# A decoder block in three-pass float32 matmuls: high and low halves share a tile, and gap tiles set their addresses

## The chip, the core and the metric

The kernel runs on one core of a Trainium2 chip. The metric is the device time of one execution in microseconds. A core has a matrix engine (TensorE, PE in the profile), a vector engine (VectorE, DVE), an activation engine (ScalarE, ACT), a general engine (GpSimd, POOL) and a queue that issues transfers (SyncE, SP). TensorE multiplies a stationary operand, the weights, which a separate step loads (PEld in the profile), with a moving operand that streams past it. Both are read from SBUF, the on-chip memory of 128 partitions; the result goes to PSUM, from which the other engines read it.

## The reference, cut to what matters

One layer of a decoder for 256 prompt tokens and 8 x 4 sample tokens, 288 in all, with a width of 2048. Everything is float32.

```python
mod = silu(c) @ w_ada + b_ada                      # shifts, scales, gates
h = rmsnorm(x, norm1) * (1 + sc1) + sh1
proj = h @ w_in                                    # 2048 -> 4632
u_pool, z, xbc, dt_raw = split(proj)
mix = concat(pool_mixer(u_pool), ssd_mixer(z, xbc, dt_raw)) @ w_out
x = x + g1 * mix
h2 = rmsnorm(x, norm2) * (1 + sc2) + sh2
up = h2 @ w_up                                     # 2048 -> 2 x 5504
act = silu(causal_dwconv(up[:, :5504])) * up[:, 5504:]
x = x + g2 * (act @ w_down)
y = rmsnorm(x, norm_f)                             # and the new states
```

## The kernel before, in words

The data lie transposed: features on the partitions, the 288 tokens along the row. A width of 2048 is 16 tiles of 128 x 288. [...] Each factor is split into a high half, rounded to float32r, and a low half, the rest. Then `mm3` (lines 222 to 226) adds three products into one PSUM bank: high weights by high operand (L224), high weights by low operand (L225), low weights by high operand (L226). Every pass has its own weight load of 128 x 128 and streams 288 columns.

The operands that move are h1 (for the input projection), mix (for the output projection) and h2 (for up); `new_operand` (lines 179 to 181) makes 16 high tiles under one tag and 16 low tiles under another, in the pool `kp`. The 43 activation tiles for down are made one by one in `up_pair` (lines 1024 to 1027), with 17 buffers for the high and 17 for the low halves.

Weights come from DRAM in pieces of 128 x 1024 on SP's queue (`load`, line 208). `split` (lines 214 to 220) makes two tiles of each piece: ACT casts it into `whi` (L218), DVE subtracts that from the piece into `wlo` (L219). The class `_W` (line 363) hands out the buffers in turn. The first pool has two of each, and a second pool adds two more of each in the output projection, when the mixer's memory has come free. A piece holds 8 blocks of 128 x 128, so it serves 24 matmuls.

Order of the stages: c and x in, the first norm; the modulation weights and the input projection (`xbc`, then `dt` with blocks of 24 columns, then `uz`), with the mixers' work woven in; the output projection (`out`); the second norm; the first three pairs of columns of up, k by k (`up`, 18 matmuls for each k); then 40 pairs `gate` and `val`, of 48 matmuls each, and in three groups `down`. A tile framework sets the semaphores: it knows which part of a tile an instruction reads or writes, and a new tile in an old buffer waits until the old one is released. A scheduler orders each engine's instructions from the dependencies and its own estimates; work marked with high priority, such as the casts and subtractions of `split`, goes ahead.

Addresses are dealt out by the pools, one tile after the other. An operand tile takes 1152 bytes of each partition, a piece of split weights 4096, a block of it 512.

Of the kernel before, what the change touches and what calls it, by code (L numbers as in the profile page):

```python
# [11 lines left out]
F32 = mybir.dt.float32  # L12
F32R = mybir.dt.float32r
# [4 lines left out]
P = 128  # L18
D = 2048
KT = D // P  # L20
# [3 lines left out]
N = NP + NS  # L24
# [13 lines left out]
WU = (14, 2, 2, 2, 6)  # L38
RAW1, RAW2 = 8, 1
SPLIT1, SPLIT2 = 2, 2  # L40
YK = 2
NX = (10, 1, 1, 1, 1)
AY = 2
# [14 lines left out]
RAWC = 1024  # L58
# [73 lines left out]
def kernel(ctx: ExitStack, tc, ins, outs):  # L132
# [4 lines left out]
    kp = ctx.enter_context(tc.tile_pool(name="kp", bufs=1))  # L137
# [38 lines left out]
    xhi = [None]  # L176
    xlo = [None]

    def new_operand(name):
        xhi[0] = [kp.tile([P, N], F32R, tag="xhi", name=f"{name}h{k}", bufs=KT) for k in range(KT)]  # L180
        xlo[0] = [kp.tile([P, N], F32R, tag="xlo", name=f"{name}l{k}", bufs=KT) for k in range(KT)]

    def col_sums(ps, src, rhs, first, last):

# [21 lines left out]
    wp = [None]  # L206

    def load(key):
        off, cols = S.items[key]
        t = wp[0].tile([P, RAWC], F32, tag="raw", name="raw_" + "_".join(map(str, key)))  # L210
        nc.sync.dma_start(t[:, :cols], wflat[off:off + P * cols].rearrange("(p n) -> p n", p=P))
        return t

    def split(raw, a, n, name):
        hi = wp[0].tile([P, RAWC], F32R, tag="whi", name="whi_" + name)
        lo = wp[0].tile([P, RAWC], F32R, tag="wlo", name="wlo_" + name)
        with tc.high_priority():
            nc.scalar.copy(hi[:, :n], raw[:, a:a + n])  # L218
            nc.vector.tensor_tensor(lo[:, :n], raw[:, a:a + n], hi[:, :n].bitcast(F32), ALU.subtract)  # L219
        return hi, lo  # L220

    def mm3(ps, whi, wlo, c, bh, bl, first, last, n=P):
        w = slice(c * n, c * n + n)
        nc.tensor.matmul(ps, whi[:, w], bh, start=first, stop=False)  # L224
        nc.tensor.matmul(ps, whi[:, w], bl, start=False, stop=False)  # L225
        nc.tensor.matmul(ps, wlo[:, w], bh, start=False, stop=last)  # L226
# [3 lines left out]
    def project_units(key, nk, opnd=None, order=None):  # L230

        name = "_".join(map(str, key))
        ps = pm.tile([P, 512], F32, tag="mm", name="mm_" + name)
        for h, (k0, n) in enumerate(_halves(nk)):
            hi, lo = ready.pop(key + (h,), None) or split(load(key + (h,)), 0, n * P, f"{name}_{h}")
            for i in range(n):
                k = k0 + i
                ko = order[k] if order else k
                bh, bl = (xhi[0][ko], xlo[0][ko]) if opnd is None else opnd(k)
                mm3(ps[:, :N], hi, lo, i, bh, bl, k == 0, k == nk - 1)  # L240
                if k % YK == YK - 1 or k == nk - 1:
                    yield ps

    def project(key, nk, opnd=None, order=None):
        for ps in project_units(key, nk, opnd, order):
            pass
        return ps
# [93 lines left out]
    def samp(ap):  # L341
        return ap.rearrange("p (b l) -> p b l", b=NB)
# [20 lines left out]
    class _W:  # L363


        def __init__(self):
            self.slots = {"raw": [], "whi": [], "wlo": []}
            self.i = {"raw": 0, "whi": 0, "wlo": 0}

        def add(self, pool, nraw, nsp):  # L370
            for tag, n in (("raw", nraw), ("whi", nsp), ("wlo", nsp)):
                m = len(self.slots[tag])
                if m:
                    r = self.i[tag] % m
                    self.slots[tag] = self.slots[tag][r:] + self.slots[tag][:r]
                    self.i[tag] = 0
                self.slots[tag] += [(pool, n)] * n
# [11 lines left out]
    for q in range(4):  # L389
        t = mx.tile([P, 4, N], F32, tag="blk", name=f"xa{q}", bufs=4)  # L390
# [36 lines left out]
    nc.vector.memset(upp[:, :, 0:15], 0.0)  # L427

    new_operand("h1")

    selr = mx.tile([P, 32], F32R, name="selr")
# [415 lines left out]
    for gi in range(len(KGROUPS)):  # L847
        last = gi + 1 == len(KGROUPS)
        if last:
            hi, lo = split(load(("dt",)), 0, KT * NH, "dt")  # L850
# [23 lines left out]
    n = 0  # L874
    zlast = 3 * (4 - ZEARLY) * KT // YK
    for m in list(range(4 + 3 * ZEARLY, 16)) + ULATE:
# [22 lines left out]


    new_operand("mix")
    def mix_pool(g):
        nc.scalar.copy(xhi[0][g], pout[0][:, g, :])
        nc.vector.tensor_tensor(xlo[0][g], pout[0][:, g, :], xhi[0][g].bitcast(F32), ALU.subtract)

    for g in range(4):
        for t in range(3):
            k = 4 + 3 * g + t
# [7 lines left out]
    ff = ctx.enter_context(tc.tile_pool(name="ff", bufs=1, reuse_waits="tile"))  # L916
    w2 = ctx.enter_context(tc.tile_pool(name="w2", bufs=1, reuse_waits="tile"))
    x = ff.tile([P, KT, N], F32, name="x")


    rt = [kp.tile([P, N], F32, tag="ssx", name="rt2")]
# [60 lines left out]
    for _ in range(GA[1]):  # L982
        next(adag2)
    new_operand("h2")
    up0 = [(pm.tile([P, 512], F32, tag="mm", name=f"mm_up{i}") if i < 3 else aux(f"mm_up{i}"))
           for i in range(2 * FK)]
    for k0, n in [(0, 1), (1, 1)] + [(k, 2) for k in range(2, KT, 2)]:
        modulate(x[:, k0:k0 + n, :], rstd2 if k0 > 1 else rstd2p, 1, 3, k0, n, f"n{k0}")
        for k in range(k0, k0 + n):
            hi, lo = ready.pop(("upk", k), None) or split(load(("upk", k)), 0, 2 * FK * P, f"upk{k}")  # L990
# [9 lines left out]
    def up_pair(j):  # L1000
        pg = up0[2 * j] if j < FK else project(("gate", j), KT)
        gb = ff.tile([P, NG], F32, tag="gb", name=f"gb{j}", bufs=2)
        gs = gb[:, 2 + NP:].rearrange("p (b l) -> p b l", b=NB)
        nc.gpsimd.memset(gb[:, 0:2], 0.0)
        nc.gpsimd.tensor_copy(gs[:, :, 0:2], stf[:, j])
        nc.scalar.copy(gb[:, 2:2 + NP], pg[:, 0:NP])
        nc.scalar.copy(gs[:, :, 2:6], samp(pg[:, NP:N]))
        nc.gpsimd.tensor_copy(nff[:, j, 0:2], gb[:, NP:NP + 2])
        nc.gpsimd.tensor_copy(nff[:, j, 2:18].rearrange("p (b l) -> p b l", b=NB), gs[:, :, 4:6])
        fw = V_FW + 3 * j  # L1010
        gc = ff.tile([P, NG], F32, tag="gc", name=f"gc{j}", bufs=2)
        nv = NG - 2
        nc.vector.tensor_scalar(gc[:, :nv], gb[:, 0:nv], vec[:, fw:fw + 1], vec[:, V_FB + j:V_FB + j + 1],
                                ALU.mult, ALU.add)
        for i in (1, 2):
            nc.vector.scalar_tensor_tensor(out=gc[:, :nv], in0=gb[:, i:i + nv], scalar=vec[:, fw + i:fw + i + 1],
                                           in1=gc[:, :nv], op0=ALU.mult, op1=ALU.add)
        nc.scalar.activation(gc[:, :nv], gc[:, :nv], AF.Silu)
        pv = up0[2 * j + 1] if j < FK else project(("val", j), KT)
        act = ff.tile([P, N], F32, tag="act", name=f"act{j}", bufs=2)  # L1020
        nc.vector.tensor_tensor(act[:, 0:NP], gc[:, 0:NP], pv[:, 0:NP], ALU.mult)
        gcs = gc[:, 2 + NP:].rearrange("p (b l) -> p b l", b=NB)[:, :, 0:NL]
        nc.vector.tensor_tensor(samp(act[:, NP:N]), gcs, samp(pv[:, NP:N]), ALU.mult)
        ah = ff.tile([P, N], F32R, tag="ah", name=f"ah{j}", bufs=17)
        al = ff.tile([P, N], F32R, tag="al", name=f"al{j}", bufs=17)
        nc.scalar.copy(ah, act)  # L1026
        nc.vector.tensor_tensor(al, act, ah.bitcast(F32), ALU.subtract)
        acts[j] = (ah, al)
# [39 lines left out]
    xf = [None]  # L1068

    def down(gi):  # L1070
        k0, nk = DGROUPS[gi]
        last = gi == len(DGROUPS) - 1
        for m in range(16):
            for i, ps in enumerate(project_units(("down", gi, m), nk, lambda k: acts[k0 + k])):
                if last and m == KT - 1 and i == 5:
                    all_but_last("ssumf")
            residual(ps, 5, m)
            if last:
                squares(m, "f")
                nc.scalar.activation(xf[0][m], x[:, m, :], AF.Identity, scale=vec[:, V_NF + m:V_NF + m + 1])  # L1080

    for gi, (k0, nk) in enumerate(DGROUPS):
        for j in range(k0, k0 + nk):
            up_pair(j)
            if gi == 0 and j >= 3:
                next(adag2, None)
                next(adag2, None)
            if j >= SM0:
                next(states, None)
            if gi and j == k0:  # L1090
                drain(adag2)
                down(gi - 1)
    drain(states)
    nc.gpsimd.dma_start(outs["o_ffn"], nff)
    rt[0] = kp.tile([P, N], F32, tag="ssx", name="rtf")
    xf[0] = [kp.tile([P, N], F32, tag="xhi", name=f"xf{m}", bufs=KT) for m in range(KT)]
    down(len(DGROUPS) - 1)


# [161 lines left out]
```

## Time and profile before

| | us |
|---|---|
| median of 3 runs | 1391.12 |
| the runs | 1389.8 to 1391.21 |
| span of the profiled execution | 1387.7 |
| median of the runs less that span | 3.4 |
| TensorE busy | 1363.0 (98%) |
| weight loads | 1252.7 (90%) |
| DVE, ACT, POOL busy | 823.0, 576.7, 228.6 |

The span runs from the first to the last instruction of the profiled execution; a run's time also holds what lies around that, so a sum against the span is carried over with the 3.4 us. A matmul's end is modelled, and matmuls overlap in the records (each is listed with some 295 ns, and the next starts some 133 ns later). So the rate of a stage is read from the distance between starts. The timeline prints starts to 10 ns; the trace holds whole nanoseconds, and means over many starts are given to a hundredth.

### The profile page before, as it was taken

The numbers are of one execution on the slowest core, as the hardware profiler recorded it, in microseconds if no ns is written. First come the engines' busy times: TensorE is split into PE (matmuls) and PEld (weight loads), VectorE is DVE, ScalarE is ACT, GpSimd is POOL, SyncE is SP. The second block draws the span as 40 slices with busy tenths as digits, with TensorE's granted clock in tenths as the row PEclk, the third lists the DMA queues.
The fourth block names the chain that finished last, engine by engine and source line by source line (L and its number), as shares of the span: only waits on it lengthen the run. The fifth ranks groups of instructions, "written<-read, shape, count | busy, mean of one in ns | idle before, by whom it ended". The sixth has DMA issues, their size and how long they took to land.

```text
span 1387.7 us, 26411 instructions
## 1 busy us (share of the span) xinstructions
PE 1363.0 (98%) x10565; PEld 1252.7 (90%) x10565; DVE 823.0 (59%) x1448; ACT 576.7 (42%) x925; POOL 228.6 (16%) x428
## 2 busy tenths in 40 slices
PE   8999999999989999999999999999999999999997
PEld 7678888777679998998999999999999999999997
DVE  3775657968774447745565445665664565565553
ACT  5222333479653334533443333434433334343452
POOL 0000000121122223111221001312120012122221
PEclk9999999999999999999999999999999999999999
DMA  8888887978788887788655555655555555556531
GB/s 340 306 296 306 307 283 253 340 278 326 296 310 316 332 286 245 219 290 280 217 180 175 170 173 180 199 190 188 180 179 167 181 191 190 188 187 197 188 118 68
DMA packets 97194, 323.20 MB, mean 233 GB/s; under 512 B 10736, under 2 KB 19888, under 8 KB 97072
## 3 DMA queue, kind: packets, MB, share of 16 engines
q1 hardware_dynamic: 93168, 310.63, 65.6%
q0 software_dynamic: 3184, 9.69, 1.9%
q8 instruction: 83, 1.36, 0.4%
q10 hardware_dynamic: 720, 1.19, 0.2%
q14 instruction: 39, 0.32, 0.1%
HBM read 309.78 MB, written 10.39 MB: 231 GB/s over the span
## 4 chain that ended last, share of the span: by engine, by line
PE 94%; DVE 3%; DMA 1%; ACT 1%; issue 0%; POOL 0%; SPq 0%; DVEq 0%; POOLq 0%; ACTq 0%
PE mm_down L224 7%; PE mm_down L226 7%; PE mm_down L225 7%; PE mm_gate L226 6%; PE mm_gate L224 6%; PE mm_val L225 6%; PE mm_gate L225 6%; PE mm_val L226 6%; PE mm_val L224 6%; PE xbc L224 5%; PE xbc L225 4%; PE xbc L226 4%; PE adap L322 3%; PE mm_out L224 3%; PE mm_out L225 3%; PE mm_out L226 2%
## 5 line engine op out<-in xcount | busy, mean ns | idle before, releaser
L224 PE MATMUL mm_down<-ah,whi_down 128*128 128x288 f32 x688 | 203.7, 296 | 0.0
L226 PE MATMUL mm_down<-ah,wlo_down 128*128 128x288 f32 x688 | 203.5, 296 | 0.0
L225 PE MATMUL mm_down<-al,whi_down 128*128 128x288 f32 x688 | 203.3, 295 | 0.0
L226 PE MATMUL mm_gate<-h2h,wlo_gate 128*128 128x288 f32 x640 | 190.2, 297 | 0.0
L224 PE MATMUL mm_gate<-h2h,whi_gate 128*128 128x288 f32 x640 | 189.8, 297 | 0.0
L225 PE MATMUL mm_gate<-h2l,whi_gate 128*128 128x288 f32 x640 | 189.3, 296 | 0.0
L225 PE MATMUL mm_val<-h2l,whi_val 128*128 128x288 f32 x640 | 188.8, 295 | 0.0
L226 PE MATMUL mm_val<-h2h,wlo_val 128*128 128x288 f32 x640 | 188.5, 295 | 0.0
L224 PE MATMUL mm_val<-h2h,whi_val 128*128 128x288 f32 x640 | 188.0, 294 | 0.0
L219 DVE TENSOR_TENSOR wlo_gate<-raw_gate,whi_gate 128x1024 fp32r<-128x1024 f32 x80 | 98.5, 1232 | 138.7 <-ACT whi_gate L218 138.6
L219 DVE TENSOR_TENSOR wlo_down<-raw_down,whi_down 128x1024 fp32r<-128x1024 f32 x96 | 107.9, 1123 | 116.8 <-ACT whi_down L218 116.0
L218 ACT CAST whi_down<-raw_down 128x1024 fp32r<-128x1024 f32 x96 | 92.2, 961 | 169.2 <-PE mm_down L225 119.2
L218 ACT CAST whi_gate<-raw_gate 128x1024 fp32r<-128x1024 f32 x80 | 83.9, 1050 | 163.4 <-PE mm_gate L225 68.8
L224 PE MATMUL xbc<-h1h,whi_xbc 128*128 128x288 f32 x448 | 139.9, 313 | 4.6 <-DVE cvp L553 2.9
L218 ACT CAST whi_val<-raw_val 128x1024 fp32r<-128x1024 f32 x80 | 84.1, 1051 | 125.6 <-issue 102.3
L225 PE MATMUL xbc<-h1l,whi_xbc 128*128 128x288 f32 x448 | 132.4, 296 | 0.3 <-DVE h1l L360 0.3
L226 PE MATMUL xbc<-h1h,wlo_xbc 128*128 128x288 f32 x448 | 131.8, 297 | 0.0
L225 PEld LDWEIGHTS mm_down<-al,whi_down 128*128 128x128 f32 x688 | 129.7, 189 | 0.0
L226 PEld LDWEIGHTS mm_down<-ah,wlo_down 128*128 128x128 f32 x688 | 129.6, 188 | 0.0
L224 PEld LDWEIGHTS mm_down<-ah,whi_down 128*128 128x128 f32 x688 | 129.6, 188 | 0.0
L224 PEld LDWEIGHTS mm_gate<-h2h,whi_gate 128*128 128x128 f32 x640 | 120.4, 188 | 5.0 <-ACT ah L1026 3.4
L225 PEld LDWEIGHTS mm_gate<-h2l,whi_gate 128*128 128x128 f32 x640 | 120.7, 189 | 0.0
(318 smaller groups left out, 3003.6 us busy)
## 6 DMA issues: line engine op xcount, KB each, us to landing
raw_adap<-wflat SPq DMA_DIRECT2D x128, 512.0 KB, 5.6
raw_gate<-wflat SPq DMA_DIRECT2D x80, 512.0 KB, 3.5
raw_val<-wflat SPq DMA_DIRECT2D x80, 512.0 KB, 3.6
raw_ada<-wflat SPq DMA_DIRECT2D x64, 512.0 KB, 5.6
raw_xbc<-wflat SPq DMA_DIRECT2D x55, 512.0 KB, 5.8
raw_down<-wflat SPq DMA_DIRECT2D x48, 512.0 KB, 3.6
raw_out<-wflat SPq DMA_DIRECT2D x32, 512.0 KB, 7.0
raw_down<-wflat SPq DMA_DIRECT2D x32, 384.0 KB, 3.1
```

What stands on the lines that cost most here:

```text
L218: nc.scalar.copy(hi[:, :n], raw[:, a:a + n])
L219: nc.vector.tensor_tensor(lo[:, :n], raw[:, a:a + n], hi[:, :n].bitcast(F32), ALU.subtract)
L224: nc.tensor.matmul(ps, whi[:, w], bh, start=first, stop=False)
L225: nc.tensor.matmul(ps, whi[:, w], bl, start=False, stop=False)
L226: nc.tensor.matmul(ps, wlo[:, w], bh, start=False, stop=last)
L322: i = nc.tensor.matmul(ps[32 * j:32 * j + 32, :512], sc_c[:, k, :], raw[:, (j % 2) * 512:(j % 2) * 512 + 512], start=(k == ay - 1), stop=( ...
```

## The change

Nothing is computed in another way. `new_operand` makes 16 tiles of 128 x 2 x 288, the high half first; `up_pair` does the same for the activations. `split` makes one tile of 2048 + 64 columns for a piece, with the high half at column 0 and the low half at column 1024 + 32. `_W` has one list of buffers for it in place of two. `shift` takes a small unused tile from a pool, so that what the pool deals out afterwards lies 192 bytes (pool `kp`, operands), 32 bytes (pool `ff`, activations) or 0 bytes (second weight pool) further on. The tiles of the final norm use the operands' buffers as before, under the new tag.

```diff
+PHASE = (192, 32, 0)
...
+    def shift(pool, n, name):
+        if n:
+            pool.tile([P, n // 4], F32, name="gap_" + name)
+
+    shift(kp, PHASE[0], "x")
+
     def new_operand(name):
-        xhi[0] = [kp.tile([P, N], F32R, tag="xhi", name=f"{name}h{k}", bufs=KT) for k in range(KT)]
-        xlo[0] = [kp.tile([P, N], F32R, tag="xlo", name=f"{name}l{k}", bufs=KT) for k in range(KT)]
+        pair = [kp.tile([P, 2, N], F32R, tag="xop", name=f"{name}k{k}", bufs=KT) for k in range(KT)]
+        xhi[0] = [t[:, 0, :] for t in pair]
+        xlo[0] = [t[:, 1, :] for t in pair]
...
     def split(raw, a, n, name):
-        hi = wp[0].tile([P, RAWC], F32R, tag="whi", name="whi_" + name)
-        lo = wp[0].tile([P, RAWC], F32R, tag="wlo", name="wlo_" + name)
+        pair = wp[0].tile([P, 2 * RAWC + 64], F32R, tag="wsp", name="wsp_" + name)
+        hi, lo = pair[:, 0:RAWC], pair[:, RAWC + 32:2 * RAWC + 32]
...
-        for tag, n in (("raw", nraw), ("whi", nsp), ("wlo", nsp)):
+        for tag, n in (("raw", nraw), ("wsp", nsp)):
...
+    shift(ff, PHASE[1], "a")
+    shift(w2, PHASE[2], "w")
...
-        ah = ff.tile([P, N], F32R, tag="ah", name=f"ah{j}", bufs=17)
-        al = ff.tile([P, N], F32R, tag="al", name=f"al{j}", bufs=17)
+        ahl = ff.tile([P, 2, N], F32R, tag="ahl", name=f"ahl{j}", bufs=17)
+        ah, al = ahl[:, 0, :], ahl[:, 1, :]
```

Two places show what this does to the instructions. The first is DVE, in the middle of gate and val, with the semaphores that each instruction waits for. Before (`wlo` is the low half of a piece of weights, `gc` the convolved gate, `act` its product with val):

```order
L219 TENSOR_TENSOR wlo_gate_0_9912<-raw_gate_0_9909,whi_gate_0_9911 128x1024 [waits DMAHW3_49,PE_49,Activation_49]
L219 TENSOR_TENSOR wlo_gate_1_9942<-raw_gate_1_9939,whi_gate_1_9941 128x1024 [waits DMAHW4_49,PE_49,Activation_49]
L1013 TENSOR_SCALAR gc_9831<-gb_9824,vec 128x304 [waits Activation_49]
L1016 SCALAR_TENSOR_TENSOR gc_9831<-gb_9824,vec,gc_9831 128x304 [waits DVE_49] x2
L219 TENSOR_TENSOR wlo_val_0_9985<-raw_val_0_9982,whi_val_0_9984 128x1024 [waits DMAHW5_49,PE_49,Activation_49]
L1021 TENSOR_TENSOR act_9897<-gc_9831,mm_val_9836 128x256 [waits PE_49,Activation_49]
```

The same place in the changed kernel, where high and low half are parts of one tile `wsp`:

```order
L228 TENSOR_TENSOR wsp_gate_0_9633<-raw_gate_0_9631,wsp_gate_0_9633 128x1024 [waits DMAHW3_49,Activation_49]
L228 TENSOR_TENSOR wsp_gate_1_9662<-raw_gate_1_9660,wsp_gate_1_9662 128x1024 [waits DMAHW4_49,Activation_49]
L1024 TENSOR_SCALAR gc_9556<-gb_9549,vec 128x304 [waits Activation_49]
L1027 SCALAR_TENSOR_TENSOR gc_9556<-gb_9549,vec,gc_9556 128x304 [waits DVE_49] x2
L228 TENSOR_TENSOR wsp_val_0_9704<-raw_val_0_9702,wsp_val_0_9704 128x1024 [waits DMAHW5_49,Activation_49]
L1032 TENSOR_TENSOR act_9620<-gc_9556,mm_val_9561 128x256 [waits PE_49,Activation_49]
```

The order is the same. The subtraction no longer waits for TensorE, since the cast ahead of it on ACT has waited for the release of the whole tile.

The second place is ACT, late in the input projection, around the step that makes dt (`csd`, `ex`, `etb`, `csr` belong to it, `cf` to the convolution). Before:

```order
L218 CAST whi_xbc_6_2849<-raw_xbc_6_2847 128x1024 [waits DMAHW3_49,Activation_49]
L506 ACTIVATE csd<-csd 128x72 [waits DVE_49]
L510 ACTIVATE ex<-csd 128x24
L511 ACTIVATE ex<-cumt 128x24 [waits PE_49]
L521 ACTIVATE etb<-totb 128x192 [waits PE_49]
L527 CAST csr<-cumr 24x288 [waits PE_49]
L218 CAST whi_xbc_7_2889<-raw_xbc_7_2887 128x1024 [waits DMAHW4_49,PE_49,Activation_49]
L570 ACTIVATE cf_3141<-cvp_161,vec 128x312 x4
L218 CAST whi_xbc_8_2945<-raw_xbc_8_2943 128x1024 [waits DMAHW1_49,DVE_49,PE_49]
```

And in the changed kernel:

```order
L227 CAST wsp_xbc_6_2784<-raw_xbc_6_2782 128x1024 [waits DMAHW3_49,DVE_49,PE_49]
L515 ACTIVATE csd<-csd 128x72 [waits DVE_49]
L519 ACTIVATE ex<-csd 128x24
L520 ACTIVATE ex<-cumt 128x24 [waits PE_49]
L227 CAST wsp_xbc_7_2823<-raw_xbc_7_2821 128x1024 [waits DMAHW4_49,PE_49,Activation_49]
L530 ACTIVATE etb<-totb 128x192
L536 CAST csr<-cumr 24x288
L579 ACTIVATE cf_3070<-cvp_162,vec 128x312 x5
L227 CAST wsp_xbc_8_2878<-raw_xbc_8_2876 128x1024 [waits DMAHW1_49,DVE_49,PE_49]
```

Here the cast of piece 7 has moved two places ahead, and the cast of piece 6 waits for PE and DVE, the readers of the whole tile whose buffer it takes. From the second column of the output projection to the end TensorE has the same order in both kernels; the moves lie in the input projection, and a few single ones on ACT and DVE behind it.

More of the change, by code (lines that the diff above doesn't have):

```diff
@@ L366, in __init__ @@
         def __init__(self):
-            self.slots = {"raw": [], "whi": [], "wlo": []}
-            self.i = {"raw": 0, "whi": 0, "wlo": 0}
+            self.slots = {"raw": [], "wsp": []}
+            self.i = {"raw": 0, "wsp": 0}
         def add(self, pool, nraw, nsp):
-            for tag, n in (("raw", nraw), ("whi", nsp), ("wlo", nsp)):
+            for tag, n in (("raw", nraw), ("wsp", nsp)):
                 m = len(self.slots[tag])
@@ L1095 @@
     rt[0] = kp.tile([P, N], F32, tag="ssx", name="rtf")
-    xf[0] = [kp.tile([P, N], F32, tag="xhi", name=f"xf{m}", bufs=KT) for m in range(KT)]
+    xf[0] = [kp.tile([P, N], F32, tag="xop", name=f"xf{m}", bufs=KT) for m in range(KT)]
     down(len(DGROUPS) - 1)
```

## The prediction

> **What bounds the kernel now.** The page comes first: the busy times, and the chain of work that ended last.
>
> ```profile
> span 1387.7 us, 26411 instructions
> PE 1363.0 (98%) x10565; PEld 1252.7 (90%) x10565; DVE 823.0 (59%) x1448; ACT 576.7 (42%) x925; POOL 228.6 (16%) x428
> PE 94%; DVE 3%; DMA 1%; ACT 1%; issue 0%; POOL 0%; SPq 0%; DVEq 0%; POOLq 0%; ACTq 0%
> ```
>
> TensorE sets the end: 98% busy and 94% of the chain. The table of stretches says where anything else could count.
>
> ```profile
> 50.00:330.00 280.00, 275.17 (x2197) 219.39 (x2197) 195.60 (x452) 111.97 (x181) 27.20 (x47) 1.00 0.83 299
> 640.00:1000.00 360.00, 360.00 (x2706) 357.40 (x2706) 206.33 (x297) 139.61 (x196) 60.14 (x130) 1.00 0.59 191
> 1000.00:1388.00 388.00, 378.19 (x2843) 377.73 (x2841) 215.11 (x327) 153.25 (x220) 69.36 (x131) 0.99 0.53 168
> ```
>
> From 640 to 1000 us TensorE is never idle (360.00 of 360.00) at a granted clock of 1.00; in the input projection, 50 to 330 us, it lacks 4.8 us. Since it is always busy, "busy" says nothing about how fast it goes. That is read from the start-to-start distance, the pitch, in the timeline. Here two neighbouring matmuls of a "val" tile, with the weight loads beside them:
>
> ```profile
> 1200.32 0.29 PE L224 MATMUL mm_val<-h2h,whi_val 128*128 128x288 f32 x1
> 1200.32 0.19 PEld L225 LDWEIGHTS mm_val<-h2l,whi_val 128*128 128x128 f32 x1
> 1200.45 0.30 PE L225 MATMUL mm_val<-h2l,whi_val 128*128 128x288 f32 x1
> 1200.45 0.19 PEld L226 LDWEIGHTS mm_val<-h2h,wlo_val 128*128 128x128 f32 x1
> ```
>
> The load of the next weights starts with the matmul before it: while TensorE streams a moving operand, it fetches the weights of the following one from the same memory. That is the pair whose distance the change sets. L224 to L226 run 2912 times each, 8736 matmuls. In 8569 cases one is followed by another; 8397 of these lie under 150 ns apart, and their mean pitch is 132.74 ns, 1114.6 us of the span.
>
> **Does the pitch depend on that distance?** Call the offset the byte address of the next weights minus that of the moving operand, modulo 256. An operand tile is 288 x 4 = 1152 bytes, 4.5 x 256, so neighbouring tiles flip the offset by 128; a block of weights is 512 bytes, so it does not move. From the allocator's addresses, the weight buffers of the first pool give 64 and 192 with h1, mix and h2, those of the second 96 and 224; in "down" the two pools give 224/96 and 0/128. The four offsets that stand still over 18 matmuls are in the first columns of up, one k after the other:
>
> ```profile
> 552.60 0.30 PE L224 MATMUL mm_up<-h2h,whi_upk 128*128 128x288 f32 x1
> 555.00 0.30 PE L224 MATMUL mm_up<-h2h,whi_upk 128*128 128x288 f32 x1
> 557.40 0.29 PE L224 MATMUL mm_up<-h2h,whi_upk 128*128 128x288 f32 x1
> 559.76 0.29 PE L224 MATMUL mm_up<-h2h,whi_upk 128*128 128x288 f32 x1
> 562.16 0.30 PE L224 MATMUL mm_up<-h2h,whi_upk 128*128 128x288 f32 x1
> ```
>
> These are the first of 18 each. Offset 224: 2.40 us, 133.3 ns each. Offset 96: 2.40, 133.3. Offset 192: 2.36, 131.1. Offset 64: 2.40, 133.3. So the pitch does depend on the offset, by some 2 ns in 133. The long tiles agree, each from its first to its last start (47, 47 and 41 pitches):
>
> ```profile
> 1115.98 0.30 PE L224 MATMUL mm_gate<-h2h,whi_gate 128*128 128x288 f32 x1
> 1122.25 0.29 PE L226 MATMUL mm_gate<-h2h,wlo_gate 128*128 128x288 f32 x1
> 1122.38 0.30 PE L224 MATMUL mm_val<-h2h,whi_val 128*128 128x288 f32 x1
> 1128.60 0.30 PE L226 MATMUL mm_val<-h2h,wlo_val 128*128 128x288 f32 x1
> 1306.86 0.30 PE L224 MATMUL mm_down<-ah,whi_down 128*128 128x288 f32 x1
> 1312.29 0.30 PE L226 MATMUL mm_down<-ah,wlo_down 128*128 128x288 f32 x1
> ```
>
> Gate (96 and 224 by turns of three) 6.27 / 47 = 133.4; val (64 and 192) 6.22 / 47 = 132.3; down at 0 and 128 by single turns 5.43 / 41 = 132.4.
>
> **The change, part by part.** *The offset.* An operand pair is now 2304 bytes, 9 x 256, low half 1152 on, which is 128 modulo 256. A weight pair is 8448 bytes, 33 x 256, low half 4224 on, again 128. High on high, low operand before low weights, high operand before the next high weights: all three have one offset, and the gaps bring it to 0, in every stage; only the 24-column dt weights still run through all values. So 8397 pairs, now 534 at 0, 2011 at 64, 1637 at 96, 509 at 128, 2021 at 192 and 1673 at 224, go to 0 (12 others lie in dt).
>
> What is the pitch at 0? It occurs in "down" alone, alternating strictly with 128, so no row of it stands alone. Between these first and last starts, 528 pitches at 0 average 131.45 ns and 503 at 128 average 134.16:
>
> ```profile
> 750.05 0.29 PE L224 MATMUL mm_down<-ah,whi_down 128*128 128x288 f32 x1
> 1374.35 0.29 PE L226 MATMUL mm_down<-ah,wlo_down 128*128 128x288 f32 x1
> ```
>
> This is the nearest row, and I take it: 132.74 - 131.46 = 1.28 ns over 8397 is **10.7 us** less. (131.46 is the mean of all 534.) It is a weak row, though. In the same lines 96 and 224 alternate and average 132.11 and 134.48, while standing alone both run at 133.3: alternation itself splits the pitch into a short and a long one, and the split may not survive. Bounds: upwards 134.16, if the delay recorded at 128 belongs to the 0 that follows, +1.42 ns, +11.9 us. Downwards the shortest pitch that recurs anywhere, 127 ns, every fourth start or so in the runs at 192, -5.74 ns, -48.2 us; it is always made up by a 135 behind it, so as a mean it is a far bound. Nearer is the dt tile, whose loads are of 24 columns only:
>
> ```profile
> 213.05 0.29 PE L224 MATMUL mm_dt<-h1h,whi_dt 128*24 128x288 f32 x1
> 219.22 0.29 PE L226 MATMUL mm_dt<-h1h,wlo_dt 128*24 128x288 f32 x1
> ```
>
> 47 pitches in 6.17 us are 131.3 ns: with hardly a load beside it, the matmul still takes 131. That is close to 131.46, and it says that a conflict with the weight load can explain only about 1.5 ns of the 132.7.
>
> [...]
>
> *The shared weight tile.* The cast on ACT (L218) used to need only its high buffer, released by the last L225 (the third row below: 76.3 us of such waits in xbc, all of it time in which TensorE works); now it needs the pair, released by the last L226, one pitch or 0.13 us later. DVE's subtraction loses its wait for PE. Queued behind the cast on ACT are the bias and SiLU steps, behind the subtraction on DVE the residuals.
>
> ```profile
> L219 DVE TENSOR_TENSOR wlo_gate<-raw_gate,whi_gate 128x1024 fp32r<-128x1024 f32 x80 | 98.5, 1232 | 138.7 <-ACT whi_gate L218 138.6
> L218 ACT CAST whi_gate<-raw_gate 128x1024 fp32r<-128x1024 f32 x80 | 83.9, 1050 | 163.4 <-PE mm_gate L225 68.8
> ACT whi_xbc L218 <- PE xbc L225: 76.3, 27, 7.1
> ```
>
> A buffer holds 8 blocks, 24 matmuls, 24 x 132.7 = 3.2 us. Cast and subtraction take 1.05 + 1.23 = 2.3 us, now 2.4 from release to use. Two buffers (input projection) leave 3.2 us for it, four (from "out" 5 on) 9.6 us. So 0, hidden by the other buffers' matmuls. If that cover were gone, the 55 chunks of xbc and 24 loads of uz would cost 79 x 0.13 = 10 us.
>
> *Order.* The scheduler puts a few instructions elsewhere in the input projection: casts on ACT stand a place to three earlier or later, dt's transposes behind 7 more matmuls. What waits of TensorE there are at L224 now is this:
>
> ```profile
> PE xbc L224 <- DVE cvp L553: 2.9, 3, 1.6
> PE xbc L224 <- ACT h1h L359: 1.6, 2, 1.3
> ```
>
> So 4.5 us could move; between -2 and +4 us, I take 0. No matmul, load or transfer is added, and an unused gap costs nothing. The 1829 other matmuls have other operands and are left as they are (at 1.28 ns each, 2.3 us).
>
> *Sum.* 1387.7 - 10.7 + 0 + 0 = 1377.0 us of span. The median of the runs, 1391.12, lies 3.4 us above the profiled span, which is what lies around it, so **1380.4 us**.
>
> **Rivals.** *The floor drops (A).* Should 0 be where the two streams never meet, the dt row says 131, but the recurring 127 says that a matmul can be quicker: 1391.1 - 48.2 = 1342.9. Against it: dt itself, 131.3 with small loads.
>
> *Nothing happens (B).* The split in "down" is made by the alternation, and 0 alone runs at the mean of the pair, 132.8: 1391. For it: 96 and 224, which split by 2.4 ns when mixed and not at all alone. [...] Against it: 192 alone is quicker than 64.
>
> *0 is a slow offset (C).* Three of the four offsets that stand alone run at 133.3, and 224, only 32 from 0, is one of them. If 0 stands with them, every pitch becomes 133.3, 0.6 ns more, 8397 x 0.6 = 5.0 us: 1396; with 134.16, 1403. Place: every L224 to L226; it decides for slower from a pitch of 133.1 on, where the quicker 192 and 64 of val have been given up for nothing. Against it: the 131.45.
>
> *The shared buffer bites (D).* Casts released later, and some standing later on ACT, leave TensorE without weights in the input projection: up to the 10 us above, against a gain of 10.7: about 1391, or up to 1401 if the pitch does not fall either. Against it: 0.9 us of slack in each turn.
>
> **How the numbers follow.** Forecast (pitch 130 to 132.3, that is 1368 to 1387.5) 0.48, A 0.14, B 0.14, C 0.19, D 0.05. The likeliest gives 1380.4. The range reaches up through B to the near end of C, 1397, and down half way to A, a pitch near 128.9, 1358. Left out are most of A and the far end of C and D, about 0.2. About 0.2%, 2.8 us or 0.33 ns of pitch, is what a measurement of this kernel can tell from no change. Faster: forecast and A, 0.62. Same: B, 0.14. Slower: C and D, 0.24.
>
> **What would show it.** Right: in the timeline of the changed kernel gate, val and down all have one and the same pitch, near 131.4, and the up columns step by 2.36 to 2.37 us for each k; the 640 to 1000 stretch holds about 1% more matmuls. The group rows of casts and subtractions keep their durations, and no wait of L224 for ACT or DVE in xbc grows past a few us. Wrong: one pitch at 133 or more (C), pitches that differ between gate and down (the addresses don't do what the change says), 127 to 130 (A), or idle time before L224 (D).

## The result, and the profile after

| | before | changed |
|---|---|---|
| median of 4 runs each, same chip, us | 1390.46 | 1380.91 |
| lowest and highest, us | 1389.26, 1391.21 | 1379.69, 1381.84 |
| ratio of the medians, 95% interval | | 0.9932 [0.9918, 0.9946] |
| span of the profiled execution, us | 1387.7 | 1379.8 |
| mean pitch of the pairs under 150 ns | 132.74 ns (8397) | 131.75 ns (8381) |

The change makes the kernel 0.68% faster, 9.6 us by the medians and 7.9 us by the two spans. In the page of the changed kernel the busy times and the chain of work that ended last read almost as before:

```profile
span 1379.8 us, 26352 instructions
PE 1358.6 (98%) x10565; PEld 1246.1 (90%) x10565; DVE 823.6 (60%) x1448; ACT 575.2 (42%) x925; POOL 232.0 (17%) x428
PE 93%; DVE 3%; DMA 1%; ACT 1%; issue 1%; POOL 0%; SPq 0%; DVEq 0%; POOLq 0%; ACTq 0%
```

The same 10565 matmuls, TensorE still 98% busy and still the bound; it is busy for a shorter time. The stretches of the changed kernel (after the length: busy time and, in brackets, instructions of PE, weight loads, DVE, ACT and POOL; then the granted clock, the share of the transfer engines and GB/s) say where:

```profile
50.00:330.00 280.00, 276.76 (x2186) 218.81 (x2187) 196.36 (x449) 110.12 (x180) 26.83 (x47) 0.99 0.84 297
640.00:1000.00 360.00, 360.00 (x2728) 357.39 (x2727) 207.39 (x300) 140.86 (x198) 59.48 (x129) 1.00 0.59 191
```

From 640 to 1000 us TensorE is never idle in either kernel, the clock is 1.00 in both, and it gets through 2728 matmuls in place of 2706. From 50 to 330 us it is 2186 in place of 2197; other matmuls stand between the pairs there, so that count doesn't measure the pitch, which fell in xbc too, from 132.27 to 131.53 ns.

The account closes in the starts of all TensorE instructions. From one three-pass matmul to the next (mm3, now lines 233 to 235), the longer gaps included, the sum was 1159.2 us and is 1150.9, 8.3 less; everything else on TensorE went from 217.6 to 218.1 us. Together that is the 7.9 us of the span. So the whole gain lies in the pitch.

But the pitch is not one pitch. These are rows of the timeline of the changed kernel: the first start of gate 30, its last, the last of val 30, then the next gate tile from its first to its last. `hs` is a pair of matmuls of the mixer's state (line 1073, 384 columns) that happens to stand between:

```profile
1108.63 0.29 PE L233 MATMUL mm_gate<-h2k,wsp_gate 128*128 128x288 f32 x1
...
1114.79 0.29 PE L235 MATMUL mm_gate<-h2k,wsp_gate 128*128 128x288 f32 x1
...
1121.08 0.30 PE L235 MATMUL mm_val<-h2k,wsp_val 128*128 128x288 f32 x1
1121.22 0.51 PE L1073 MATMUL hs<-xm,bm 128*128 128x384 f32 x2
1121.56 0.29 PE L233 MATMUL mm_gate<-h2k,wsp_gate 128*128 128x288 f32 x1
...
1127.83 0.30 PE L235 MATMUL mm_gate<-h2k,wsp_gate 128*128 128x288 f32 x1
```

Gate 30 takes 6.16 us for 47 pitches, 131.1 ns each. After `hs`, the next gate tile takes 6.27 / 47 = 133.4, with every operand and every weight at the same offset 0. It stays so, tile after tile, until the next `hs` 26 us later, and then goes back. The trace's whole nanoseconds give 131.11 and 133.33 ns for these two courses, "quick" and "slow" below; all of output projection, up and the first two groups of down are quick, the third group of down is slow from end to end, and gate and val change sides at each of the 14 `hs` pairs that stand by themselves, from 708 to 1263 us, by strict turns. Some 2100 of the 8381 pairs run slow; at 2.2 ns each that is 4.6 us which the change could have had and did not get.

Not every foreign matmul turns the course. Between 582 and 641 us five groups of 16 matmuls of the modulation (line 331) stand between a val and the next gate tile, and the 94 pairs behind each average 131.10 ns, quick as before; behind a sixth group, of 8 at 655 us, they average 133.37.

The other terms of the sum, in the groups and waits of the changed kernel:

```profile
L228 DVE TENSOR_TENSOR wsp_gate<-raw_gate,wsp_gate 128x1024 fp32r<-128x1024 f32 x80 | 98.0, 1226 | 137.6 <-ACT wsp_gate L227 137.6
L227 ACT CAST wsp_gate<-raw_gate 128x1024 fp32r<-128x1024 f32 x80 | 83.9, 1050 | 162.2 <-PE mm_gate L235 71.3
L233 PE MATMUL xbc<-h1k,wsp_xbc 128*128 128x288 f32 x448 | 139.6, 313 | 3.5 <-ACT h1k L368 1.7
ACT wsp_xbc L227 <- PE xbc L235: 67.7, 25, 4.0
```

Subtraction and cast take 1226 and 1050 ns, as before (1232, 1050). The cast in xbc now waits for the last L235 of the pair, 67.7 us in all in place of 76.3. TensorE's own wait at the first pass in xbc is 3.5 us, 4.6 before.

### The profile page after: what moved, and what is told of

Same layout as the page of the kernel before. It is cut to its first block, busy times and chain, and to the rows that moved or that the text cites. A ratio compares the mean times of both kernels' runs of the same rounds, so it can differ in the third digit from the quotient of the medians.

```text
span 1379.8 us, 26352 instructions
## 1 busy us (share of the span) xinstructions
PE 1358.6 (98%) x10565; PEld 1246.1 (90%) x10565; DVE 823.6 (60%) x1448; ACT 575.2 (42%) x925; POOL 232.0 (17%) x428
## 4 chain that ended last, share of the span: by engine, by line
PE 93%; DVE 3%; DMA 1%; ACT 1%; issue 1%; POOL 0%; SPq 0%; DVEq 0%; POOLq 0%; ACTq 0%
PE mm_down L234 7%; PE mm_down L235 7%; PE mm_down L233 7%; PE mm_val L234 6%; PE mm_gate L234 6%; PE mm_gate L233 6%; PE mm_val L235 6%; PE mm_gate L235 6%; PE mm_val L233 6%; PE xbc L233 5%; PE xbc L234 4%; PE xbc L235 4%; PE adap L331 4%; PE mm_out L234 3%; PE mm_out L233 3%; PE mm_out L235 2%
## 5 line engine op out<-in xcount | busy, mean ns | idle before, releaser
L234 PE MATMUL mm_down<-ahl,wsp_down 128*128 128x288 f32 x688 | 204.3, 297 | 0.0
L235 PE MATMUL mm_down<-ahl,wsp_down 128*128 128x288 f32 x688 | 202.8, 295 | 0.0
L233 PE MATMUL mm_down<-ahl,wsp_down 128*128 128x288 f32 x688 | 202.1, 294 | 0.0
L234 PE MATMUL mm_val<-h2k,wsp_val 128*128 128x288 f32 x640 | 190.1, 297 | 0.0
L234 PE MATMUL mm_gate<-h2k,wsp_gate 128*128 128x288 f32 x640 | 190.0, 297 | 0.0
L235 PE MATMUL mm_val<-h2k,wsp_val 128*128 128x288 f32 x640 | 188.8, 295 | 0.0
L235 PE MATMUL mm_gate<-h2k,wsp_gate 128*128 128x288 f32 x640 | 188.8, 295 | 0.0
L233 PE MATMUL mm_gate<-h2k,wsp_gate 128*128 128x288 f32 x640 | 188.8, 295 | 0.0
L233 PE MATMUL mm_val<-h2k,wsp_val 128*128 128x288 f32 x640 | 188.0, 294 | 0.0
L228 DVE TENSOR_TENSOR wsp_gate<-raw_gate,wsp_gate 128x1024 fp32r<-128x1024 f32 x80 | 98.0, 1226 | 137.6 <-ACT wsp_gate L227 137.6
L228 DVE TENSOR_TENSOR wsp_down<-raw_down,wsp_down 128x1024 fp32r<-128x1024 f32 x96 | 107.3, 1118 | 121.9 <-ACT wsp_down L227 121.0
L227 ACT CAST wsp_down<-raw_down 128x1024 fp32r<-128x1024 f32 x96 | 92.2, 960 | 167.3 <-PE mm_down L235 116.8
L227 ACT CAST wsp_gate<-raw_gate 128x1024 fp32r<-128x1024 f32 x80 | 83.9, 1050 | 162.2 <-PE mm_gate L235 71.3
L233 PE MATMUL xbc<-h1k,wsp_xbc 128*128 128x288 f32 x448 | 139.6, 313 | 3.5 <-ACT h1k L368 1.7
L234 PE MATMUL xbc<-h1k,wsp_xbc 128*128 128x288 f32 x448 | 133.4, 298 | 0.3 <-DVE h1k L369 0.3
L235 PE MATMUL xbc<-h1k,wsp_xbc 128*128 128x288 f32 x448 | 132.6, 298 | 0.1
L233 PEld LDWEIGHTS mm_down<-ahl,wsp_down 128*128 128x128 f32 x688 | 129.6, 188 | 0.0
L234 PEld LDWEIGHTS mm_down<-ahl,wsp_down 128*128 128x128 f32 x688 | 129.3, 188 | 0.0
L235 PEld LDWEIGHTS mm_down<-ahl,wsp_down 128*128 128x128 f32 x688 | 129.2, 188 | 0.0
L233 PEld LDWEIGHTS mm_gate<-h2k,wsp_gate 128*128 128x128 f32 x640 | 120.5, 188 | 5.0 <-ACT ahl L1037 4.2
L233 PEld LDWEIGHTS mm_val<-h2k,wsp_val 128*128 128x128 f32 x640 | 120.6, 188 | 0.0
```

## The experiments

**The theories.** (1) *Distance*: what counts is the offset of the next weights from the moving operand modulo 256; 0 is quick, others are not. (2) *Sameness*: the pitch was long because the offset alternated; any single offset will do. (3) *Tiles*: the gain comes from the shared tiles, with their waits and order, and not from addresses.

Eight of the kernels below differ from the changed one in nothing but the three gap sizes. In seven of them `PHASE` = (192 + d, 32, 256 - d) moves every operand by d and leaves the weights of both pools where they were modulo 256, so that all offsets become 256 - d; the program is otherwise the same. The eighth has no gaps. Each kernel has one profile, off192 two. "Pitch" is the mean of the mm3 pairs under 150 ns, some 8385 in each; the ratio is to the kernel before, run beside it.

### One half of the period away, and a quarter to each side

```diff
-PHASE = (192, 32, 0)
+PHASE = (320, 32, 128)      # off128: every pair at 128
+PHASE = (384, 32, 64)       # off64: every pair at 64
+PHASE = (256, 32, 192)      # off192: every pair at 192
```

> The changed kernel with other gap tiles, so that every pair of moving operand and next weights stands 128 bytes apart modulo 256 in place of 0; pairing of the halves, instructions and waits are those of the changed kernel. Theory 1, the offset 0 itself is the quick one (before, 128 averaged 134.16 ns in down against 131.45 at 0): mean pitch 133.3 to 134.2 ns, 8381 pairs x 1.6 to 2.4 = 13 to 20 us above the changed kernel, 1394 to 1401 us. Theory 2, what helps is that the offset no longer alternates, at whatever value: mean pitch 131.7, 1381 us. Theory 3, the gain came from the shared weight tile (fewer waits), not from the pitch at all: 1381 us as well, with the pitch free.

> The changed kernel with every pair 64 bytes apart modulo 256. Theory 1, by the value that stood alone before (133.3 ns at 64): mean pitch 133.3, 13 us above the changed kernel, 1394 us. Theory 2, uniformity: 131.7 and 1381 us.

> The changed kernel with every pair 192 bytes apart modulo 256. Theory 1, by the value that stood alone before (131.1 to 131.7 ns at 192): mean pitch 131.1 to 131.7, within 5 us of the changed kernel, 1376 to 1381 us. Theory 2, uniformity: 131.7 and 1381 us. Here both say nearly the same; the run shows whether 0 is a special value or one of several quick ones.

| every pair at | median us (runs) | ratio [95%] | span | pitch |
|---|---|---|---|---|
| 128 | 1391.97 (10) | 1.0017 [1.0007, 1.0026] | 1389.3 | 133.24 |
| 64 | 1384.03 (3) | 0.9955 [0.9940, 0.9971] | 1382.2 | 132.23 |
| 192 | 1376.72 (2) | 0.9903 [0.9883, 0.9923] | 1375.6 | 131.53 |

The 640 to 1000 us stretch, of off128, off64 and off192 in turn:

```profile
640.00:1000.00 360.00, 360.00 (x2699) 357.40 (x2698) 207.02 (x297) 139.72 (x196) 60.06 (x130) 1.00 0.59 190
```

```profile
640.00:1000.00 360.00, 360.00 (x2720) 357.39 (x2719) 208.94 (x301) 139.82 (x198) 58.84 (x128) 1.00 0.59 191
```

```profile
640.00:1000.00 360.00, 360.00 (x2738) 357.41 (x2737) 208.97 (x300) 140.68 (x198) 58.50 (x129) 1.00 0.60 193
```

The same program gets through 2699, 2720 or 2738 matmuls in 360 us, and only addresses differ. That refutes theories 2 and 3: at 128 everything is as even as at 0, and all tiles are shared, and the gain is gone; the interval even lies above 1, since the quick pairs of the kernel before have been given up as well. Theory 1 holds, but not with 0 as the best: 192 beats it. Nor do its figures hold throughout: 128 stayed under the 133.3 to 134.2 ns expected of it, and 64, at 132.2, fits neither the 133.3 of theory 1 nor the 131.7 of theory 2. At 192 the slow course does not appear behind `hs`; the 5211 pairs from 670 us on average 131.2 ns. Its loss lies earlier: from 330 to 566 us, output projection and the up columns, it runs at 132.3 to 132.6.

### The odd multiples of 32

```diff
+PHASE = (224, 32, 224)      # off224
+PHASE = (288, 32, 160)      # off160
+PHASE = (416, 32, 32)       # off32
+PHASE = (352, 32, 96)       # off96
```

> The changed kernel with every pair 224 bytes apart modulo 256, between the quick values 192 and 0. Theory 1, by the value that stood alone before (133.3 ns at 224): mean pitch 133.3, 1394 us. Theory 2, uniformity: 131.7 and 1381 us. A third reading, that the pitch runs smoothly with the offset: near 131.5.

> The changed kernel with every pair 160 bytes apart modulo 256. Theory 1, each offset has its own pitch, and the quick ones lie around 192 and 0: 160 lies between 192 (131.53 ns in the run before) and 128 (133.25), so by a smooth course 132.3 ns and 1384 us. Against that the few pairs at 160 in dt, 12 to 18 in all the traces so far, average 129 to 131 ns: by those rows 130 ns, 8380 x 1.5 = 13 us under the run at 192, 1364 us. Theory 2, only the remainder modulo 64 matters (0 and 192 quick by chance): 160 stands with 224 and 96, 133.3 ns, 1392 us.

> The changed kernel with every pair 32 bytes apart modulo 256. Theory 1 as a smooth course between 0 (131.75) and 64 (132.23): 132.0 ns, 1382 us. Theory 2, the remainder modulo 64 decides and 32 stands with 224: 133.3 ns, 1392 us.

> The changed kernel with every pair 96 bytes apart modulo 256. By the value that stood alone before the change, 133.3 ns, 1392 us, with either theory; a pitch under 132.5 would say that what stood alone over 18 matmuls is no guide to a uniform kernel.

| every pair at | median us (runs) | ratio [95%] | pitch |
|---|---|---|---|
| 224 | 1392.15 (8) | 1.0016 [1.0006, 1.0026] | 133.29 |
| 160 | 1391.41 (10) | 1.0013 [1.0003, 1.0022] | 133.25 |
| 32 | 1392.36 (8) | 1.0015 [1.0005, 1.0026] | 133.28 |
| 96 | 1391.95 (8) | 1.0017 [1.0005, 1.0028] | 133.29 |

All four are slow from end to end, and slow means the same 133.3 as at 128. The 130 ns that a few pairs at 160 in dt had suggested did not appear. So there is no smooth course with a best place: 32 bytes beside the quick 0 or 192 lies the full loss. Of the eight steps of 32 only 0, 64 and 192 have a quicker course at all.

### Distance, or the operand's own address?

In the kernels so far the operands moved, and the first weight pool did not. Here the operands stay, and the halves of the weights start 128 bytes further on in their tile:

```diff
-        hi, lo = pair[:, 0:RAWC], pair[:, RAWC + 32:2 * RAWC + 32]
+        hi, lo = pair[:, 32:RAWC + 32], pair[:, RAWC + 64:2 * RAWC + 64]   # w128
```

> The changed kernel with operands and gap tiles as they are, and both halves of the weights 128 bytes further on inside their tile: every pair 128 bytes apart, as in the earlier run at 128, but with the operands at the addresses that ran at offset 0. In the runs so far the operands were moved and the weights stood still. Theory 1, the distance of the two decides: mean pitch 133.2 to 133.3 ns, 1391 to 1392 us, no gain over the kernel before. Theory 2, the operand's own address decides: 131.75 ns, 1381 us.

1391.36 us (10 runs), ratio 1.0016 [1.0007, 1.0026], pitch 133.26: all of off128's loss, with the operands where the change put them. From 640 to 1000 us it makes the same 2699 matmuls as off128:

```profile
640.00:1000.00 360.00, 360.00 (x2699) 357.40 (x2698) 205.08 (x296) 139.55 (x196) 59.49 (x128) 1.00 0.59 190
```

Neither the operand's address nor that of the weights decides alone, since moving either of them by 128 brings the same loss; the distance decides. The hybrid kernel below is the converse: in its early stages both are moved by 64, the distance is 0 again, and the pitch is quick (131.26 ns from 330 to 540 us).

### The shared tiles without the gaps

```diff
-PHASE = (192, 32, 0)
+PHASE = (0, 0, 0)           # nogap
```

> The changed kernel without its gap tiles: the halves still share their tiles, so the three products of a step still have one offset, but it is 192 in xbc and uz, 192 or 224 in out and up, 224 in gate, 192 in val, and 0 or 224 by turns of a piece in down. If the uniform kernels' pitches add up by share (4041 pairs at 192 with 131.6, 3293 at 224 with 133.3, 1031 at 0 with 131.75): mean pitch 132.3, 4.6 us above the changed kernel, 1385.5 us. If the pairing alone brought the gain: 1381 us. If the gap tiles alone brought it: 1390 us.

1385.94 us (8 runs), ratio 0.9972 [0.9960, 0.9983], pitch 132.54. Sharing the tiles takes the alternation away by itself, and leaves the offsets at 192, 224 and, in part of down, 0. By offset, the trace gives 131.09 ns at 0 (1037 pairs), 132.35 at 192 (4005) and 133.24 at 224 (3304). The gaps, which bring everything to 0, are thus worth the step from 0.9972 to 0.9932, more than half of the gain.

### What sets quick or slow at offset 0?

If a foreign matmul shifts the course, one put in on purpose should do it too. The last group of down, slow throughout in the changed kernel, gets an extra matmul of 288 columns ahead of columns 0, 4, 8 and 12 (in the trace the first one stands behind the fifth matmul of column 0). Its result is used by nothing; the output stays the same, and the kernel does four matmuls more.

```diff
+            if last and m % 4 == 0:
+                kick = aux(f"kick{m}")
+                tc.keep_in_program_order(nc.tensor.matmul(kick[:, :N], acts[k0][0][:, 0:P],
+                                                          acts[k0 + 1][0], start=True, stop=True))
```

> The changed kernel (offset 0) with four extra matmuls of 288 columns into an unused bank, one ahead of each fourth column of the last group of down; they add work and change no address. In the changed kernel this group ran at 133.33 ns throughout, the group before it at 131.11, with the same offset. Theory A, at one offset TensorE's two read streams can lock in two ways, and any break in the sequence picks one: the pitch of the last group changes at one or more of the four places, 133.33 to 131.11 or back, 165 pairs x 2.2 = 0.37 us for each stretch that turns quick, against 4 x 0.13 us of added work. Theory B, something else slows the last group (the buffers' addresses, the final sums beside it): 133.33 ns throughout, and 0.5 us longer.

In the timeline of that kernel, the first and the last start of column 3, the extra matmul, the first start of column 4 and its last; then the next extra matmul, and the first and the last start of column 8:

```profile
1291.75 0.29 PE L233 MATMUL mm_down<-ahl,wsp_down 128*128 128x288 f32 x1
...
1297.12 0.29 PE L235 MATMUL mm_down<-ahl,wsp_down 128*128 128x288 f32 x1
1297.26 0.29 PE L1087 MATMUL kick<-ahl,ahl 128*128 128x288 f32 x1
1297.38 0.30 PE L233 MATMUL mm_down<-ahl,wsp_down 128*128 128x288 f32 x1
...
1302.85 0.30 PE L235 MATMUL mm_down<-ahl,wsp_down 128*128 128x288 f32 x1
...
1319.78 0.30 PE L1087 MATMUL kick<-ahl,ahl 128*128 128x288 f32 x1
1319.92 0.29 PE L233 MATMUL mm_down<-ahl,wsp_down 128*128 128x288 f32 x1
...
1325.30 0.29 PE L235 MATMUL mm_down<-ahl,wsp_down 128*128 128x288 f32 x1
```

Column 3 (the first two starts shown) takes 5.37 us for 41 pitches, 131.0; column 4, behind the extra matmul, 5.47, 133.4; column 8, behind the next one, 5.38, 131.2. Columns 0 to 3 and 8 to 11 are quick, 4 to 7 and 12 to 15 slow: every one of the four changed the course, two of them to quick and two to slow. From gate on, up to this group, the kernel repeats the courses of the changed one, with the turns at the same 14 `hs` pairs. Two stretches between them show that nothing else differs:

```profile
1281.00:1297.00 16.00, 16.00 (x125) 16.00 (x124) 7.79 (x12) 8.25 (x12) 3.58 (x6) 1.00 0.60 186
1298.00:1314.00 16.00, 16.00 (x122) 16.00 (x121) 7.42 (x11) 7.78 (x12) 3.94 (x6) 1.00 0.58 173
```

Clock, transfers and the other engines are as good as equal; TensorE does 125 matmuls in one and 122 in the other. The kernel as a whole took 1380.11 us, in a single run. So quick and slow are two stable courses of the same stream, and an interruption can turn the one into the other; stage and column do not set them. Both occur at offset 0 in one group of columns, so the slow one is not a matter of another distance.

### The best of both

Since 0 is quick in the early stages and can turn slow later, and 192 the other way round, one more kernel takes each where it is quick: the gaps of off192, and the weights of the stages ahead of gate and val 64 bytes further on in their tile, which brings those stages back to 0.

```diff
-PHASE = (192, 32, 0)
+PHASE = (256, 32, 192)
...
-        hi, lo = pair[:, 0:RAWC], pair[:, RAWC + 32:2 * RAWC + 32]
+        o = 0 if name[:4] in ("gate", "val_", "down") else 16
+        hi, lo = pair[:, o:o + RAWC], pair[:, o + RAWC + 32:o + 2 * RAWC + 32]
```

> The kernel at 192, with the weights of the early stages (xbc, uz, out, the first columns of up) put 64 bytes further on in their tile, so that these stages run at offset 0 and gate, val and down at 192. In the runs at one offset, 0 gave 131.1 to 131.7 ns in the early stages and 192 gave 132.0 to 132.4 there, while from gate on 192 gave 131.1 to 131.3 and 0 gave 131.8 to 132.0. If the pitch follows the offset of the pair alone, stage by stage: 1153 x 0.65 + 296 x 0.3 + 737 x 1.3 + 282 x 1.3 = 2.2 us under the kernel at 192, 1374.5 us. If the way a stage locks depends on what came before as much as on the offset: between 1374 and 1381 us, with some stages at 132.6 or 133.3.

It ran beside a repetition of off192:

> The kernel with every pair 192 bytes apart once more, for a narrower interval. If its mean pitch of 131.53 ns is a property of the addresses, the span is within 1 us of 1375.6 again and the ratio to the kernel before 0.990; the changed kernel had 0.9932.

| | median us (runs) | ratio [95%] | pitch |
|---|---|---|---|
| hybrid | 1376.34 (4) | 0.9904 [0.9887, 0.9920] | 131.42 |
| off192 again | 1377.42 (4) | 0.9914 [0.9900, 0.9929] | 131.43 |

The early stages follow as meant: from 330 to 540 us the pairs average 131.26 in the hybrid, 132.3 in the first off192. The next stretch takes it back: the first gate and val tiles, 566 to 670 us, run at 132.5 in the hybrid and at 131.6 in off192. That is the second of the two readings that were put down for it. And off192 itself does not repeat its courses: in the second profile the output projection averaged 131.32 ns, in the first 132.39, and the span is 1374.2 us in place of 1375.6. From 395 to 525 us the first and the second profile of off192 read:

```profile
395.00:525.00 130.00, 127.19 (x951) 111.62 (x950) 64.95 (x110) 47.97 (x70) 27.72 (x39) 0.99 0.80 297
395.00:525.00 130.00, 127.21 (x956) 110.26 (x954) 63.61 (x111) 47.89 (x69) 27.86 (x38) 0.99 0.80 296
```

So hybrid and off192 can't be told apart. Both beat the kernel before by 0.9 to 1.0%; off192 lies below the changed kernel's 0.9932 in both measurements, though the intervals overlap. Where a stretch is all quick, no run here shows more to gain in this way: no kernel had a stage with a mean under 131.0.

## Why the prediction was right, and where it was not

**The total.** 1380.4 us predicted, 1380.9 measured. Two misses cancel in it, and that they do is luck. The span was to be 1377.0 and is 1379.8. The 3.4 us added for what lies around it were too much: in each run of the record, time and span lie 1.7 to 1.9 us apart. The 3.4 were the distance of one execution from the median of other ones, and so held their scatter too; the changed kernel's profiled execution, 1381.55 us, lies above its median, and there the distance is 1.1.

**The offset.** The step that carried the forecast held: the distance modulo 256 decides, off128 against off192 (133.24 and 131.53 ns) and w128 against the changed kernel (133.26 and 131.75) show it, and an equal 0 is quicker than the mixture (131.75 against 132.74). Between off128 and off192 it is 2699 against 2738 matmuls in the same 360 us, with nothing changed but the addresses.

**Its size.** The term was 8397 x 1.28 = 10.7 us and measured 8.3. The pitch at 0 had been read as 131.46, the mean of starts that alternated with another offset; it is 131.75, and 0.29 x 8381 = 2.4 us is what the span lacks, with the 0.4 us outside the pairs. The number came close without being the thing, and this too is luck: the changed kernel runs at 131.1 or at 133.3, and 131.75 is how the turns happened to share it out. So the sentence of the prediction that gate, val and down would have "one and the same pitch, near 131.4" is wrong: their means are 131.96, 131.95 and 131.82, and each is a mixture. It was right for the output projection (131.08) and for up, where the first pass steps like this in the changed kernel, six triples apart:

```profile
544.86 0.29 PE L233 MATMUL mm_up<-h2k,wsp_upk 128*128 128x288 f32 x1
547.22 0.29 PE L233 MATMUL mm_up<-h2k,wsp_upk 128*128 128x288 f32 x1
549.58 0.29 PE L233 MATMUL mm_up<-h2k,wsp_upk 128*128 128x288 f32 x1
551.94 0.29 PE L233 MATMUL mm_up<-h2k,wsp_upk 128*128 128x288 f32 x1
```

2.36 us for 18 matmuls, each time. The count from 640 to 1000 us rose by 0.8%, near the 1% foreseen.

**The rows that stood alone.** Over 18 matmuls, 224 and 96 at 133.3 and 192 at 131.1 were what the uniform kernels gave (133.29, 133.29, and 131.1 as the quicker of 192's courses). The fourth, 64 at 133.3, was not: with all pairs at 64 it is 132.2. A pitch read behind a change of offset may be that of a course which the change started. The same goes for the reading that "alternation itself splits the pitch": the split 131.46 and 134.16 did not survive, as it said might happen, and the 134 at 128 became 133.25.

**The rivals.** A, the floor drops: no. The dt tile, with loads of 24 columns, shows 131.4 in the changed kernel and 131.2 to 131.9 in all of them, and no stage of a uniform offset came below 131.0; the recurring 127 is made up, as the prediction said: in the changed kernel 454 of 474 such pitches inside the three-pass stream are followed by one of 133 or 134 ns. B, nothing happens: refuted by the ratio; with an offset such as 128 (ratio 1.0017) it would have been nearly right. C, 0 is a slow offset: wrong for 0, but this is what five of the eight offsets do, and its price was too high: 133.25 to 133.3 ns give 1391.4 to 1392.4 us, not 1396. By the pairs alone 0.5 ns over 8390 of them would be 4.3 us, but the medians lie only some 2 us above those of the kernel before beside them. D, the shared buffer bites: no; casts and subtractions keep their times, and the waits in xbc fell. The terms of 0 for the shared tile and for the order held as far as single profiles can show: what TensorE does outside the three-pass matmuls took 217.6 us before and 218.1 in the changed kernel, but 215.3 to 217.3 in the kernels that differ from it by gaps alone. Why this part varies by some 3 us is open.

**What stays open.** Why 0, 64 and 192 have quicker courses and the other offsets not; whether 256 bytes is the right period, which was the author's choice and which no run tested by a shift of 256 alone; what makes the two courses; and what decides which one follows a break. At 0 each single `hs` pair and each extra matmul turned the course, but only one of the six modulation groups between val and gate tiles did; at 192 the same `hs` pairs turned nothing (131.2 ns from 670 us on). Nor is it shown that an offset which was slow throughout here has no quick course. No run here looks into that.

## What to carry to other kernels

Where TensorE is 98% busy the pitch is the thing to read, tile by tile: a mean over a stage can hide two courses, as that of gate, 131.96 ns, hid tiles at 131.1 and at 133.3. When moving operand and next weights come from the same memory, try the distance between them as a number of its own, in steps of 32 bytes and by experiment, since neighbours of a good distance can be as bad as any: here 133.3 ns at 224 and at 32, beside 131.1 at 0. And repeat a pitch taken from a few alternating pairs with a kernel in which everything has that distance, before a sum is built on it.

## What the runs showed of the hardware

- The pitch of a float32r matmul of 288 columns with a load of 128 columns depends on the distance of its operand from the next weights modulo 256: in these kernels 131.1 or 133.3 ns at 0, 132.2 at 64, 131.1 or some 132.6 at 192, 133.3 at 32, 96, 128, 160 and 224.
- One stream at one distance has two stable courses. In the changed kernel the timeline shows them as stretches of equal length:

```profile
1176.00:1196.00 20.00, 20.00 (x153) 20.00 (x152) 10.87 (x16) 8.03 (x13) 4.54 (x11) 1.00 0.60 195
1202.00:1222.00 20.00, 20.00 (x155) 20.00 (x154) 13.59 (x20) 9.08 (x14) 8.94 (x11) 1.00 0.68 220
```

  153 matmuls against 155, at a clock of 1.00 in both; the quick one is the stretch with the busier DVE and the heavier transfers, so neither of these makes the slow one.
- Three passes, one block of the product, take three of these pitches: 393.3 ns in the quick course at 0 and 192, 396.7 at 64, 397.8 in the slower course at 192 and 400.0 in the slow course at 0 and at the other offsets.
- No stage here came under a mean of 131.0 ns for a matmul of 288 columns, not with loads of 24 columns either: dt ran at 131.2 to 131.9. What sets that value, no run here shows.
